# Experts' input of a hybrid decoder: plain column order, two DVE operations a tile

## The chip, the cores and the metric

The kernel runs on one core of one Trainium2 chip. The metric is the device time of one execution in microseconds (us), the median of several runs. The engines are named as in the profile: PE (TensorE), PEld (its weight loads), DVE (VectorE), ACT (ScalarE), POOL or GpSimd, and SP (SyncE), which here only issues DMAs.

## What is computed

One inference step of two trunk layers for 576 tokens of width 1024: 512 of a prompt and 64 of eight samples. The reference, cut to the part around the change:

```python
def trunk(x, c, pos0, s_gla, s_ret, s_ssd, s_conv, p):
    ...
    for l in range(DEPTH):
        mod = jax.nn.silu(c) @ p['w_ada'][l] + p['b_ada'][l]
        sh1, sc1, g1, sh2, sc2, g2 = jnp.split(mod[:, None, :], 6, axis=-1)
        h = x * (1.0 + sc1) + sh1
        mix, st = mixer(h, pos0, s_gla[l], s_ret[l], s_ssd[l], s_conv[l], l, p)
        x = layer_norm(ALPHA * x + g1 * mix, p['ln1_g'][l], p['ln1_b'][l]).astype(x.dtype)
        h = x * (1.0 + sc2) + sh2
        x = layer_norm(ALPHA * x + g2 * hier_moe(h, l, p), p['ln2_g'][l], p['ln2_b'][l]).astype(x.dtype)
    ...
```

`hier_moe` takes `h`, chooses for each token one of four groups and in it two of four experts by router logits, and adds the two experts' `(silu(h @ w1) * (h @ w3)) @ w2`, weighted. `w1` and `w3` are 1024x256, `w2` is 256x1024, all fp32. The change touches how `h`, the experts' input, is made from `x` and how `w1` and `w3` are laid out in SBUF for it.

## The kernel before

The 576 tokens lie in five tiles of rows, `t` = 0 to 3 with 128 prompt rows each and `t` = 4 with the 64 sample rows, taken in the order 4, 0, 1, 2, 3. A layer has four stages: the mixer (phase A), then phase B with the second half of the output projection, the layer norm and the router, then the experts in 16 blocks, then the combination.

In phase B each tile goes through these steps. `out_part` multiplies with the output weights on PE, and DVE applies the gate (L1576) and adds the residual with a running sum (L1580). `stat` makes the mean, the variance (ACT squares, L1610; the last tile by DVE's statistics, L1616) and the reciprocal root by DVE on single columns (L360 to L366). `experts_in` makes the experts' input `h`: ACT normalizes (L1632), GpSimd multiplies with one row vector (L1633) and adds another (L1634), each over the tile's 1024 columns; of the last tile, t = 3, ACT and GpSimd take half the columns, and DVE the other half by two fused operations (L1637, L1638). The row vectors, `r2` and `r3` in `rows`, hold the layer norm's and the modulation's factors put together; `load_rows` loads them once for tile 4 and once for the four others, into the same two buffers (`bufs=1`). The result goes into the tile `h2p`, or, for t = 0 and 2, into part of `g1`, and is stored to DRAM in `hbuf` twice by SP (L1640). The views in `experts_in` make the columns of `h` strided: column 8p + k of `x` goes to place 128k + p, so that a 128-column chunk of `hbuf` holds every eighth column.

Beside it the router works: `turn` transposes a tile (PE L1653, ACT copies into `h2T`, L1654), `logits` multiplies with the router's weights (L1660; tiles 0 to 3 straight from `x` with `wm`, tile 4 from its `h2p` with `wr`, loaded at L1513 in the matching layout), `choose` and `weigh` (L1125 to L1138 and L1148 to L1154) pick experts and weights on DVE with operations of some 16 columns, and `hot` (L1161), `rank`, `ranked` (L1696) and `weights` (L1686 to L1690) build tables that say which rows each expert takes. `srci` (L1815) holds these row numbers; the experts' blocks gather their rows of `hbuf` by it (an indirect DMA of GpSimd, L1324). Among all this, `gate` and `slots` operations of the mixer's retention heads (L1008, L1009, L1056) are fitted in.

In the experts, `expert_piece` (L1288) loads `w1`, `w3` and `w2` of a block, 1 MB each, on SP. `w1` and `w3` are loaded with "(p k) n -> p k n": a partition takes eight neighbouring rows of the weight, 8 KB in one piece, which fits the strided order of `h`. The first loads of a layer are issued in phase B, the others as their buffers come free. Some blocks split the weights into a rounded and a rest part on ACT and DVE (L329, L330), seven are used as they are.

The order of the instructions on each engine is set by the tile framework's scheduler from the program's order and its dependencies, with a few places fixed by `tc.issue_after`; each engine runs its list in order.

Of the kernel before, what the change touches and what calls it, by code (L numbers as in the profile page):

```python
# [13 lines left out]
AF = mybir.ActivationFunctionType  # L14
ALU = mybir.AluOpType
# [6 lines left out]
KD = 8  # L22
# [26 lines left out]
ORDER = (4, 0, 1, 2, 3)  # L49
# [112 lines left out]
def _body(nc, tc, a, ctx, dbg):  # L162
    pe, dve, act, pool, sp = nc.tensor, nc.vector, nc.scalar, nc.gpsimd, nc.sync
# [35 lines left out]
    def ps(cols=512, pl=None):  # L199
        if pl is None:  # L200
            turns[0] += 1
            pl = psx if turns[0] % 7 > 4 and not held else psp
        return pl.tile([128, cols], F32, name="ps", tag="ps")
# [170 lines left out]
    def tp_(t):  # L374
        return 128 if t < 4 else 64
# [907 lines left out]
    def expert_piece(l, e, i, w):  # L1283

        nm = ("moe_w1", "moe_w3", "moe_w2")[i]
        src = a[nm][l, e] if isinstance(e, int) else a[nm][l, bass.ds(e, 1)].rearrange("o a b -> (o a) b")
        nk = 2 if i == 2 else KD
        sp.dma_start(w.rearrange("p (k n) -> p k n", k=nk), src.rearrange("(p k) n -> p k n", p=128))  # L1288

    def expert_w(l, e, out):  # L1290

        for i, w in enumerate(out):
            expert_piece(l, e, i, w)
        return list(out)
# [204 lines left out]
    def phase_b(l, gates, nrm, gst, slots, rqk, rv, x, R, tabs, rst, fill):  # L1499
# [10 lines left out]
        load_mod_rows(g1, l, 0, 0)  # L1510
        load_mod_rows(g1, l, 0, 1)
        wr = rp.tile([128, KD, 20], F32, name="wr")
        sp.dma_start(wr, a["wr"][l, 0])  # L1513
        br = rp.tile([128, 20], F32, name="br")
        load_row(br, a["br"][l:l + 1, :])
        tp = mkpool(rst, "tB")
# [68 lines left out]
        rows = {}  # L1585
# [8 lines left out]
        stats, hps = {}, {}  # L1594
# [28 lines left out]
        def experts_in(t):  # L1623

            n, r = tp_(t), int(t == 4)
            mu, rstd, b = stats[t]
            views = [hps[t][:n].rearrange("q k p -> q p k")]
            views += [v[:n].rearrange("q (p k) -> q p k", k=KD) for v in (x[:, t], rows[r, 2], rows[r, 3])]

            c = 128 if t != ORDER[-1] else 64  # L1630
            hv, xv, ra, rb = [v[:, 128 - c:] for v in views]
            act.activation(hv, xv, AF.Identity, scale=rstd, bias=b)  # L1632
            pool.tensor_tensor(hv, hv, ra, op=ALU.mult)  # L1633
            pool.tensor_tensor(hv, hv, rb, op=ALU.add)  # L1634
            if t == ORDER[-1]:
                hv, xv, ra, rb = [v[:, :64] for v in views]
                dve.scalar_tensor_tensor(hv, xv, mu, ra, op0=ALU.add, op1=ALU.mult)  # L1637
                dve.scalar_tensor_tensor(hv, hv, rstd, rb, op0=ALU.mult, op1=ALU.add)  # L1638
            for o in (128 * t, PL + 128 * t):
                sp.dma_start(hbuf[o:o + n], hps[t][:n].rearrange("q k p -> q (k p)"))  # L1640

# [136 lines left out]
        p = ps(256)  # L1778
# [9 lines left out]
        for i, t in enumerate(ORDER):  # L1788
            if i + 1 < NT:
                advance(0, ORDER[i + 1])  # L1790
                nxt = out_turn(ORDER[i + 1], (0, 1))
            out_part(t, turned, ws, False, (lambda: turn((0, 1, 2)[i - 2])) if i > 1 else None)
            turned = nxt
            for _ in range(2):
                next(fill, None)
            if i == 2:
                chosen(0)
                turn(4)
            stat(t)
            experts_in(t)  # L1800
            advance(2)
            if i > 1:
                chosen((4, 1, 2)[i - 2])
            for u in ((), (), (), (0, 4), (1,))[i]:
                ranked(u)
        advance(1000)
        t = ORDER[-1]
# [13 lines left out]
    def experts(last, finish, l, x, R, tabs, slots, rqk, rv, ahead):  # L1821
# [8 lines left out]
        with ExitStack() as sE:  # L1830
# [82 lines left out]
            def load(b, i):  # L1913
                if b not in ids:
                    ids[b] = sp.value_load(tabs[2][0:1, NX + 3 + b:NX + 4 + b], min_val=0, max_val=NE - 1)
                if i == 0:
                    bl[b].w = room(b)
                expert_piece(l, ids[b], i, bl[b].w[i])
# [44 lines left out]
            with tc.If((flags & (LIGHTS | 7 << NXS)) > 0):  # L1963
                for b in LIGHT:
                    with bit(b):
                        e = sp.value_load(tabs[2][0:1, NX + 3 + b:NX + 4 + b], min_val=0, max_val=NE - 1)
                        for i in range(3):
                            expert_piece(l, e, i, w3rd[i])
                        whole(bx[b], w3rd)
                        if b in SECOND:  # L1970
                            second, third = [nc.values_load(tabs[2][0:1, i:i + 1], min_val=0, max_val=2 ** NE - 1) for i in (NX + 1, NX + 2)]
                            with tc.If((second & (1 << b)) > 0):
                                whole(b2[b], w3rd)
                            if b in THIRD:
                                with tc.If((third & (1 << b)) > 0):
                                    whole(b3[b], w3rd)
# [214 lines left out]
    with ExitStack() as sX:  # L2191
        xp = mkpool(sX, "xA")
        x = xp.tile([128, NT, D], F32, name="x")
# [15 lines left out]
    for l in range(L):  # L2209
        with ExitStack() as sL:  # L2210
# [3 lines left out]
            x = xp.tile([128, NT, D], F32, name="x")  # L2214
# [9 lines left out]
            with ExitStack() as rst:  # L2224
                fill = chain(*[ada_steps(*g) for g in MODS_B[l]])
                last, finish = phase_b(l, gates, nrm, gst, slots, rqk, rv, x, R, tabs, rst, fill)
                gst.close()
# [10 lines left out]
            with ExitStack() as sG:  # L2238
                tiles = combine(x, tail, rv, sG, LEADS[l], l + 1 == L)
                next(tiles)  # L2240
                if l + 1 < L:
# [5 lines left out]
                    for t, mu, rstd, b, o, load in tiles:  # L2247
                        n = tp_(t)
# [6 lines left out]
                    for t in ORDER:  # L2255
                        n = tp_(t)
# [3 lines left out]
                else:  # L2260
# [3 lines left out]
                    for t, mu, rstd, b, o, load in tiles:  # L2264
                        n = tp_(t)
# [6 lines left out]
                        for h in range(2):  # L2272
                            c = slice(512 * h, 512 * (h + 1)) if t == 3 else slice(0, D)
# [76 lines left out]
```

## Time and profile before

| what | us |
|---|---|
| median of 3 runs | 1425.58 (1424.96 to 1429.27) |
| profiled execution, its own time | 1436.62 |
| its span | 1434.8 |
| PE busy in the span | 1246.4 (87%) |
| DVE busy | 827.1 (58%) |
| ACT busy | 490.7 (34%) |
| POOL busy | 477.4 (33%) |

The mean granted clock of TensorE was 0.916 of full speed. The shares are averages over all stages; phase B of the first layer lies at about 403 to 474 us, that of the second at 1083 to 1155 us, and in these the shares are others, as the rows further down show. A row of a timeline gives an instruction's start and duration, and in brackets how long the engine was idle before it and which instruction ended that. A group of rows gives the busy time of many alike and their mean duration; a mean well above the shortest of them says that some were held.

### The profile page before, as it was taken

How to read it: one execution, taken by the hardware profiler on the slowest of the kernel's cores; microseconds unless marked ns; L12 is line 12 of the kernel's file. 1: busy time of each engine (PE TensorE's matmuls, PEld its weight loads, DVE VectorE, ACT ScalarE, POOL GpSimd, SP SyncE). 2: the span in 40 equal slices, each digit the busy share in tenths (PEclk: the TensorE clock that was granted, in tenths of full speed). 3: DMA queues.
4: the chain of work that ended last, by engine and by line, in shares of the span. 5: the costliest groups of instructions: out<-in, count | busy, mean ns of one | idle time of the engine just before them, and what ended most of it. 6: DMA issues, size and time to landing. Idle time of an engine off the chain costs nothing. (4 is left out here: it accounts for less than half of the span.)

```text
span 1434.8 us, 21937 instructions
## 1 busy us (share of the span) xinstructions
PE 1246.4 (87%) x8166; PEld 945.6 (66%) x8166; DVE 827.1 (58%) x1871; ACT 490.7 (34%) x909; POOL 477.4 (33%) x389
## 2 busy tenths in 40 slices
PE   4999999998987678989979998899898768998894
PEld 0999677676765455667469977777476536656651
DVE  0577457336879433446776746544687953334457
ACT  0553123332344213444345323333134421333343
POOL 0013112125244455541341312232413443534315
PEclk7899999999987699989999998999998769999897
DMA  9544665856162477986624410014555246776644
GB/s 323 169 148 158 227 231 188 293 204 205 38 193 103 161 278 296 379 319 217 189 95 149 120 60 30 5 60 161 185 191 190 101 175 249 306 289 265 213 148 139
DMA packets 100606, 267.24 MB, mean 186 GB/s; under 512 B 30871, under 2 KB 59449, under 8 KB 81528
## 3 DMA queue, kind: packets, MB, share of 16 engines
q1 hardware_dynamic: 84600, 246.62, 48.6%
q0 software_dynamic: 15872, 18.89, 4.0%
q8 instruction: 77, 1.26, 0.4%
q14 instruction: 57, 0.47, 0.1%
HBM read 246.84 MB, written 47.63 MB: 205 GB/s over the span
## 5 line engine op out<-in xcount | busy, mean ns | idle before, releaser
L403 PE MATMUL ps<-whi,hT 128*128 128x256 f32 (+1 forms) x640 | 190.0, 297 | 7.8 <-ACT hT L494 7.0
L404 PE MATMUL ps<-wlo,hT 128*128 128x256 f32 (+1 forms) x640 | 184.4, 288 | 1.2 <-DVE wlo L330 1.2
L405 PE MATMUL ps<-whi,hT 128*128 128x256 f32 (+1 forms) x640 | 184.1, 288 | 0.2
L403 PEld LDWEIGHTS ps<-whi,hT 128*128 128x128 f32 (+1 forms) x640 | 118.2, 185 | 22.1 <-issue 11.2
L404 PEld LDWEIGHTS ps<-wlo,hT 128*128 128x128 f32 (+1 forms) x640 | 118.2, 185 | 3.8 <-issue 2.1
L405 PEld LDWEIGHTS ps<-whi,hT 128*128 128x128 f32 (+1 forms) x640 | 118.1, 185 | 1.8 <-DVE hT L495 0.9
L1386 POOL DMA_INDIRECT ybuf<-ys,srci x36 | 46.8, 1300 | 134.1 <-issue 53.8
L393 PE MATMUL ps<-hT,whi 128*128 128x288 f32 x512 | 88.7, 295 | 0.0
L330 DVE TENSOR_TENSOR wlo<-wraw,whi 128x2048 fp32r<-128x2048 f32 x30 | 68.6, 2287 | 34.8 <-ACT whi L329 34.6
L330 DVE TENSOR_TENSOR wlo<-w3rd,whi 128x2048 fp32r<-128x2048 f32 x22 | 69.5, 3160 | 24.5 <-ACT whi L329 24.5
L1355 PE MATMUL ps<-whi,xh 128*128 128x256 f32 x384 | 59.0, 299 | 23.3 <-ACT xh L1342 12.7
L393 PEld LDWEIGHTS ps<-hT,whi 128*128 128x128 f32 x512 | 74.7, 188 | 0.4 <-ACT zdt L532 0.4
L1564 PE MATMUL ps<-whi,mh 128*128 128x512 f32 (+1 forms) x160 | 71.5, 447 | 3.7 <-ACT mh L1550 3.7
L266 PE MATMUL ada<-wada,scond 128*32 128x512 f32 x384 | 57.0, 668 | 18.1 <-DMA wada<-w_ada 18.1
L1565 PE MATMUL ps<-wlo,mh 128*128 128x512 f32 (+1 forms) x160 | 70.9, 443 | 0.0
L1355 PE MATMUL ps<-wlo,xh 128*128 128x256 f32 x384 | 60.0, 304 | 11.5 <-DVE wlo L330 11.4
L1355 PEld LDWEIGHTS ps<-whi,xh 128*128 128x128 f32 x384 | 52.0, 202 | 27.1 <-ACT xh L1342 13.6
L1566 PE MATMUL ps<-whi,ml 128*128 128x512 f32 (+1 forms) x160 | 68.3, 431 | 1.8 <-DVE ml L1551 1.8
L843 POOL TENSOR_TENSOR qh<-qx,ex 128x256 f32<-128x256 f32 x32 | 31.3, 1008 | 99.3 <-issue 82.0
L1355 PEld LDWEIGHTS ps<-wlo,xh 128*128 128x128 f32 x384 | 54.0, 210 | 14.8 <-DVE wlo L330 14.6
L329 ACT ACTIVATE whi<-wraw 128x2048 fp32r<-128x2048 f32 x30 | 57.3, 1911 | 12.7 <-PE ps L393 7.7
L1375 PE MATMUL ps<-w3rd,hid 128*128 128x512 f32 x128 | 58.6, 601 | 2.8 <-ACT hid L1366 2.8
(560 smaller groups left out, 2908.8 us busy)
## 6 DMA issues: line engine op xcount, KB each, us to landing
wada<-w_ada SPq DMA_DIRECT2D x48, 1024.0 KB, 5.1
wraw<-moe_w SPq DMA_DIRECT2D x36, 1024.0 KB, 9.3
slots<-moe_w SPq DMA_DIRECT2D x30, 1024.0 KB, 10.1
w3rd<-moe_w SPq DMA_DIRECT2D x30, 1024.0 KB, 12.9
wraw<-w_in SPq DMA_DIRECT2D x22, 1024.0 KB, 5.3
wraw<-w_out SPq DMA_DIRECT2D x8, 1024.0 KB, 4.9
ybuf<-bz SPq DMA_DIRECT2D x8, 512.0 KB
hbuf<-g SPq DMA_DIRECT2D x8, 512.0 KB, 2.6
```

The costliest lines, as they stand in the source:

```text
L266: pe.matmul(acc[32 * q:32 * q + 32, :], sc_[:, k, :], w[:, o:o + 512], start=(k == 0), stop=(k == KD - 1))
L329: split.hi = act.activation(hi[:, :n], raw[:, :n], AF.Copy)
L330: dve.tensor_tensor(lo[:, :n], raw[:, :n], hi[:, :n].bitcast(F32), op=ALU.subtract)
L393: pe.matmul(p[:mw, :], lhs[:, k, m0:m0 + mw], rhs[:, k, 288 * h:288 * (h + 1)], start=(k == 0 and lhs is vh and rhs is hT[0]), stop=(k == ...
L403: pe.matmul(p[:n], hT[0][:, k, xs], vh[:, k, :], start=(k == 0), stop=False)
L404: pe.matmul(p[:n], hT[0][:, k, xs], vl[:, k, :], start=False, stop=False)
L405: pe.matmul(p[:n], hT[1][:, k, xs], vh[:, k, :], start=False, stop=(k == KD - 1))
L1355: pe.matmul(p, x[:, k], v[:, k], start=(x is self.xh and v is vh and k == 0), stop=(x is self.xl and k == KD - 1))
L1375: pe.matmul(p, self.hT[:, f], v[:, f, c], start=(f == 0), stop=(f == 1))
L1564: pe.matmul(p[:n], mh[:, k, :n], vh, start=(k == 0), stop=False)
L1565: pe.matmul(p[:n], mh[:, k, :n], vl, start=False, stop=False)
L1566: o = pe.matmul(p[:n], ml[:, k, :n], vh, start=False, stop=(k == 3))
```

## The change

`experts_in` makes `h` in plain column order, by two DVE operations over the tile's 1024 columns: (x + mu) times the first row vector, then times the reciprocal root plus the second. ACT's L1632, GpSimd's L1633 and L1634 and the two half-width DVE operations go. Since `h` is in plain order, `w1` and `w3` are loaded with "(k p) n -> p k n", where a partition takes eight rows of 1 KB that lie 128 rows apart (`w2` stays as it is), and tile 4's router weights come from the copy in plain layout, of the same size. The names "first two expert weights" in the change's title mean `w1` and `w3` of every expert.

```diff
--- before.py
+++ after.py
@@ -1285,7 +1285,7 @@
         nm = ("moe_w1", "moe_w3", "moe_w2")[i]
         src = a[nm][l, e] if isinstance(e, int) else a[nm][l, bass.ds(e, 1)].rearrange("o a b -> (o a) b")
         nk = 2 if i == 2 else KD
-        sp.dma_start(w.rearrange("p (k n) -> p k n", k=nk), src.rearrange("(p k) n -> p k n", p=128))
+        sp.dma_start(w.rearrange("p (k n) -> p k n", k=nk), src.rearrange("(p k) n -> p k n" if i == 2 else "(k p) n -> p k n", p=128))
 
     def expert_w(l, e, out):
 
@@ -1510,7 +1510,7 @@
         load_mod_rows(g1, l, 0, 0)
         load_mod_rows(g1, l, 0, 1)
         wr = rp.tile([128, KD, 20], F32, name="wr")
-        sp.dma_start(wr, a["wr"][l, 0])
+        sp.dma_start(wr, a["wr"][l, 1])
         br = rp.tile([128, 20], F32, name="br")
         load_row(br, a["br"][l:l + 1, :])
         tp = mkpool(rst, "tB")
@@ -1624,18 +1624,9 @@
 
             n, r = tp_(t), int(t == 4)
             mu, rstd, b = stats[t]
-            views = [hps[t][:n].rearrange("q k p -> q p k")]
-            views += [v[:n].rearrange("q (p k) -> q p k", k=KD) for v in (x[:, t], rows[r, 2], rows[r, 3])]
-
-            c = 128 if t != ORDER[-1] else 64
-            hv, xv, ra, rb = [v[:, 128 - c:] for v in views]
-            act.activation(hv, xv, AF.Identity, scale=rstd, bias=b)
-            pool.tensor_tensor(hv, hv, ra, op=ALU.mult)
-            pool.tensor_tensor(hv, hv, rb, op=ALU.add)
-            if t == ORDER[-1]:
-                hv, xv, ra, rb = [v[:, :64] for v in views]
-                dve.scalar_tensor_tensor(hv, xv, mu, ra, op0=ALU.add, op1=ALU.mult)
-                dve.scalar_tensor_tensor(hv, hv, rstd, rb, op0=ALU.mult, op1=ALU.add)
+            hv = hps[t][:n].rearrange("p k n -> p (k n)")
+            dve.scalar_tensor_tensor(hv, x[:n, t], mu, rows[r, 2][:n], op0=ALU.add, op1=ALU.mult)
+            dve.scalar_tensor_tensor(hv, hv, rstd, rows[r, 3][:n], op0=ALU.mult, op1=ALU.add)
             for o in (128 * t, PL + 128 * t):
                 sp.dma_start(hbuf[o:o + n], hps[t][:n].rearrange("q k p -> q (k p)"))
 
```

The change also moves instructions, since the scheduler orders them anew. On DVE it puts L1628 and L1629 of each tile among the steps of the reciprocal root and the projection's residual. The first place is DVE in layer 0 where tile 0's statistics are ready (`g_3271` is tile 0's place for `h`, `r_3997` its first row vector, `mix` the gated projection, L1655 the router's logits). Before:

```order
L1609 TENSOR_SCALAR stat<-sums 128x1
L1576 TENSOR_TENSOR mix<-ps,g_3271 128x512
L360 TENSOR_SCALAR rq<-stat 128x1
L1580 SCALAR_TENSOR_TENSOR x,sums<-mix,x 128x512
L362 TENSOR_SCALAR rq<-rq 128x1
```

After:

```order
L1629 SCALAR_TENSOR_TENSOR h2p<-h2p,stat,r_3878 64x1024
L351 TENSOR_TENSOR slots<-slots 128x4
L1551 TENSOR_TENSOR ml<-ps,mh 128x512
L352 SCALAR_TENSOR_TENSOR slots<-slots 128x4
L360 TENSOR_SCALAR rq<-stat 128x1
L1628 SCALAR_TENSOR_TENSOR g_3271<-x,stat,r_3997 128x1024
L353 SCALAR_TENSOR_TENSOR slots<-slots 128x4
L362 TENSOR_SCALAR rq<-rq 128x1
L1576 TENSOR_TENSOR mix<-ps,g_3271 128x512
L351 TENSOR_TENSOR slots<-slots 128x4
L363 TENSOR_SCALAR rq<-rq 128x1
L1580 SCALAR_TENSOR_TENSOR x,sums<-mix,x 128x512
```

Tile 4's L1629 and tile 0's L1628 now stand ahead of tile 1's gate L1576 and residual L1580. Tile 4's L1628 stands 29 rows ahead of tile 0's. Tile 2's pair stands ahead of tile 3's last L1580; tile 3's pair stands behind it, where L1637 and L1638 stood.

The second place is ACT in layer 0 around the transposed copies `h2T` of tile 0 (128x512) and tile 4 (128x4x64). Before:

```order
L1610 ACTIVATE g_3271,stat<-x,stat 128x1024
L1654 ACTIVATE h2T<-ps 128x512 x2
L1632 ACTIVATE g_3271<-x,stat 128x128x8
L1854 ACTIVATE x<-x,stat 128x1024
L1654 ACTIVATE h2T<-ps 128x4x64 x2
L1610 ACTIVATE h2p,stat<-x,stat 128x1024
```

After:

```order
L1610 ACTIVATE g_3271,stat<-x,stat 128x1024
L1845 ACTIVATE x<-x,stat 64x1024
L1645 ACTIVATE h2T<-ps 128x512 x2
L1645 ACTIVATE h2T<-ps 128x4x64 x2
L1550 ACTIVATE mh<-ps 128x512
L1610 ACTIVATE h2p,stat<-x,stat 128x1024
```

L1632 of tile 0 and one other operation (`x<-x,stat`, which normalizes `x` in place for the combination) stood between the two tiles' copies; they are next to each other now.

The third place is SP in phase B of layer 0, where tile 0's row vectors (`r`) are loaded. Before:

```order
L1109 DMA ret_p<-slots 128x1x64 x2
L1288 DMA slots<-moe_w 128x2048
L315 DMA r_3998<-mrow_83 128x512 x2
L1640 DMA hbuf<-h2p 64x1024 x2
L315 DMA r_4001<-mrow_83 128x512 x2
```

After:

```order
L1109 DMA ret_p<-slots 128x1x64
L315 DMA r_3997<-mrow_83 128x512 x2
L1109 DMA ret_p<-slots 128x1x64
L1288 DMA slots<-moe_w 128x8x256
L1631 DMA hbuf<-h2p 64x1024 x2
L315 DMA r_4000<-mrow_83 128x512 x2
```

The first row vector's load now stands ahead of one store of the retention state (`ret_p`) and of one weight load, which is also one with 1 KB rows (128x8x256). GpSimd's list is the old one less the twenty rows of L1633 and L1634, and PE's keeps its order but for small moves.

## Rows read from the trace of the kernel before

**Rows 1.** Busy us by stretch: PE, PEld, DVE, ACT, POOL; clock; DMA share; GB/s

```profile
403.00:451.00 48.00, 40.85 (x222) 33.01 (x221) 43.71 (x185) 23.33 (x36) 20.11 (x8) 0.89 0.49 155
451.00:474.20 23.20, 9.90 (x58) 8.04 (x56) 22.53 (x105) 9.09 (x16) 9.09 (x4) 0.60 0.23 91
...
1131.50:1154.70 23.20, 9.50 (x60) 7.51 (x60) 22.42 (x105) 9.45 (x16) 9.11 (x4) 0.65 0.23 91
```

**Rows 2.** DVE, layer 0: start us, us, operation, idle before and releaser

```profile
423.61 0.69 DVE L1580 SCALAR_TENSOR_TENSOR x<-mix,x 128x512 f32<-128x512 f32 x1
...
453.32 2.70 DVE L1580 SCALAR_TENSOR_TENSOR x<-mix,x 128x512 f32<-128x512 f32 x1
...
455.95 2.79 DVE L1154 TENSOR_TENSOR route<-route,e 128x1 f32<-128x1 f32 x1
...
464.25 0.41 DVE L1161 TENSOR_SCALAR gate<-iota,route 128x384 bf16<-128x384 f32 x1
...
469.47 0.17 DVE L1130 TENSOR_TENSOR em<-lg,t 128x16 f32<-128x16 f32 x1
...
472.35 0.15 DVE L1154 TENSOR_TENSOR route<-route,e 128x1 f32<-128x1 f32 x1
472.42 0.22 DVE L1696 TENSOR_TENSOR A<-route,cst 128x64 bf16<-128x64 f32 x1
...
474.10 0.15 DVE L1815 SCALAR_TENSOR_TENSOR srci<-ps,tabs 128x2 int32<-128x2 f32 x1
```

**Rows 3.** GpSimd (POOL), the same columns

```profile
455.56 3.17 POOL L1634 TENSOR_TENSOR g<-g,r 128x1024 f32<-128x1024 f32 x1
```

**Rows 4.** DVE, both layers: groups by line and shape, busy us, mean ns

```profile
L1580 DVE SCALAR_TENSOR_TENSOR x<-mix,x 128x512 f32<-128x512 f32 x16 | 17.2, 1076 | 0.0
...
L1008 DVE TENSOR_TENSOR slots<-slots 128x256 f32<-128x256 f32 x8 | 6.9, 865 | 0.0
...
L1696 DVE TENSOR_TENSOR A<-route,cst 128x64 bf16<-128x64 f32 x8 | 6.9, 862 | 0.0
L1125 DVE SCALAR_TENSOR_TENSOR t<-em,m,cst 128x16 f32<-128x16 f32 x16 | 6.9, 430 | 0.1
L1130 DVE TENSOR_TENSOR em<-lg,t 128x16 f32<-128x16 f32 x8 | 6.5, 817 | 0.1
L1154 DVE TENSOR_TENSOR route<-route,e 128x1 f32<-128x1 f32 x8 | 6.5, 807 | 0.0
...
L1161 DVE TENSOR_SCALAR gate<-iota,route 128x384 bf16<-128x384 f32 x8 | 5.9, 734 | 0.0
L1696 DVE TENSOR_TENSOR A<-route,cst 64x64 bf16<-64x64 f32 x2 | 5.8, 2906 | 0.0
...
L1134 DVE SCALAR_TENSOR_TENSOR em<-route,em 128x16 f32<-128x16 f32 x8 | 3.9, 494 | 0.0
...
L1637 DVE SCALAR_TENSOR_TENSOR h2p<-x,stat,r 128x512 f32<-128x512 f32 x2 | 2.2, 1086 | 0.0
```

**Rows 5.** line L2271: duration ns min/median/max, first, last start

```profile
L2271 DVE SCALAR_TENSOR_TENSOR x<-x,cst,ln x2: 1266/1718/2170, 1416.6 to 1424.8; 128x1024 f32<-128x1024 f32 x2
```

**Rows 6.** waits, 403 to 476 us (total, times, longest); landing of `r`

```profile
PE ps L1660 <- ACT h2T L1654: 4.5, 1, 4.5
...
DMA to landing us min/median/max: 5.8/5.8/5.8
```

**Rows 7.** queue q1, 661 to 665 us (1 KB rows), 548 to 558

```profile
q1 hardware_dynamic: 1346, 1.36, 103.1%
...
q1 hardware_dynamic: 520, 3.83, 91.8%
```

**Rows 8.** PE's waits, 480 to 690 us, the longest entry

```profile
PE ps L1355 <- ACT xh L1342: 6.3, 2, 3.3
```

**Rows 9.** busy time by stretch, columns as in rows 1

```profile
490.00:520.00 30.00, 24.06 (x138) 15.83 (x138) 14.38 (x8) 9.24 (x15) 23.09 (x13) 0.83 0.96 358
...
580.00:610.00 30.00, 29.77 (x212) 20.82 (x207) 14.42 (x13) 14.01 (x19) 16.10 (x12) 1.00 1.02 399
```

## The prediction

> **What bounds the kernel now.** I read the page first, then busy time by stretch, then the two engines' own timelines over the first layer's phase B, then the groups by line over both layers. The change touches one stage of each layer (about 403 to 474 us and 1083.5 to 1155 us) and the weight loads of the expert stage behind it. In the stretch that ends the stage, DVE is busy 22.53 of 23.2 us in layer 0 and 22.42 in layer 1, PE 9.90 and ACT and POOL 9.09 each [rows 1]: DVE sets its end. In the 48 us ahead of it DVE is busy 43.71 and PE 40.85 [rows 1]; there DVE has 4.3 us of slack and either can be the one that is late. The stage ends when DVE writes `srci` at 474.10 [rows 2], which the experts' gather needs.
>
> But DVE's busy time there is not all work. L1154, one multiply of 128x1, takes 2.79 us from 455.95 and 0.15 us at 472.35 [rows 2]. It ends at 458.74; GpSimd's L1634 runs 455.56 to 458.73 [rows 3]. The DVE instruction was held until GpSimd's was done, and the same happens to a DVE instruction wherever one of GpSimd's ten LN operations of a layer runs. The groups over both layers give the size, each less its clean duration [rows 2, 4]: L1580 17.2 - 16 x 0.69 = 6.2 us; L1696 6.9 - 8 x 0.22 = 5.1 and, for 64 rows, 5.8 - 2 x 0.22 = 5.4; L1154 6.5 - 8 x 0.15 = 5.3; L1130 6.5 - 8 x 0.17 = 5.1; L1161 5.9 - 8 x 0.41 = 2.6; L1134, priced clean as L1130, 3.9 - 1.4 = 2.5; L1125, priced as L1696, 6.9 - 3.5 = 3.4; L1008, priced clean as half of L1580 and a little (0.41), 6.9 - 3.3 = 3.6. Together 39.2 us, 19.6 a layer.
>
> **The change part by part.**
>
> *GpSimd's 20 operations go.* 19.6 us of held time leave DVE in each layer, if nothing else of GpSimd takes their place: the order shows that GpSimd loses just those rows. Of this 7.2 us lie in the last stretch, behind the last tile's output projection (one of L1580, 2.70 us at 453.32 [rows 2], so 2.0; one of L1154, 2.6; L1161 and L1134, half of their two layers' 2.6 and 2.5), and 12.4 in the 48 us ahead.
>
> *DVE gets two operations a tile.* Ten of 128x1024 a layer come, and the two half-width ones of 1.09 us go [rows 4]. The nearest row with scalar operand and one tensor each of x and a row vector is L2271, 128x1024: 1.27 us clean, 2.17 for the one that was held [rows 5]. I take 1.27, since GpSimd has nearly nothing left in the stage. Ten cost 12.7 us, less 2.2: +10.5 a layer. Of these, eight operations (tiles 4, 0, 1, 2) stand in the order ahead of the last tile's residual, 10.2 us, and the last tile's pair grows by 0.4 in the last stretch. If each were held once as L2271's second was, it would be 9 us more; nothing in the order would do that to all.
>
> *ACT loses five operations a layer.* ACT is not the bound (9.09 of 23.2 [rows 1]), but in its order one of them and one other stand between tile 0's and tile 4's copies of `h2T`; PE waited 4.5 us there for tile 4's [rows 6]. After, these copies stand next to each other. I count nothing for it, since tile 4's input now comes from DVE and may be as late; up to 4.5 us a layer is the other end.
>
> *The row vectors.* `r2` and `r3` of tiles 0 to 3 are loaded into the buffers that tile 4 used, by SP after the last reader of each. The reader moves from GpSimd to DVE, and DVE now waits itself: L1628 of tile 0 for `r2`, L1629 for `r3`, with the output projection's residual and `ml` queued behind it, and PE behind those. The load takes 5.8 us from issue to landing [rows 6]. L1628 of tile 4 stands 29 rows ahead of L1628 of tile 0 in DVE's order, which hold two residuals and their sums and other 512-wide work, some 7 to 8 us. So it should be there, with a store ahead of it in SP's queue as the only doubt. I take 0, with up to 4 us a layer as the other end.
>
> *Stores of `hbuf` and SP.* The stores keep their order on SP; what they wait for ends with DVE's second operation of a tile rather than GpSimd's. The last one comes 0.4 us later behind the same DVE rows and earlier in all; nothing.
>
> *The weights.* All 64 loads of `w1` and `w3` (32 a layer) turn from 8 KB rows to 1 KB rows, and `wr` keeps its size. A load of 1 KB rows alone on the queue: 1346 packets at 103.1% of 4 us of 16 engines, 66.0 engine-us, 0.049 us a packet, 1024 packets over 16 engines 3.1 us a load [rows 7]. For 8 KB rows: 3.83 MB at 91.8% of 10 us, 146.9 engine-us, so 1.05 MB in 2.5 us [rows 7]. The difference is 0.6 us a load, 38 us of queue time over the kernel. On the path it is nothing as long as loads land before they are used: of PE's waits in the first expert stage the longest entry is one for ACT's `xh`, 6.3 us, and no weight's DMA is among them [rows 8]. The engines' time on DMA is full in two bursts a layer (0.96 of 490 to 520, 1.02 of 580 to 610) [rows 9]. A burst of 30 us at 399 GB/s is some 12 loads, eight of them `w1` or `w3`: at most 8 x 0.6 = 4.8 us late a burst, 19 us over four bursts, if nothing is loaded ahead. I take 0, since nobody waits for a load now.
>
> The rows put a 1 KB row at 3.1 / 2.5 = 1.24 of the time of the same bytes in 8 KB rows. The Trainium skill, page "DMA: Bandwidth & Descriptors", section "Why small descriptors are slow (HBM only)", names a fixed overhead of some 3 cycles a packet beside one for each 32 bytes. By it the ratio would be (35/32) / (259/256) = 1.08, an estimate from that page, a load 0.2 us longer and the four bursts at most 6 us. The trace doesn't agree; the sum goes by the rows.
>
> *Sum.* If DVE sets the pace all through, a layer gains 19.6 - 10.5 = 9.1 us. If PE does ahead of 451 us, only the last stretch counts: 7.2 - 0.4 = 6.8. I take 8.3 a layer, nearer to the first, since DVE is the busier of the two there; 16.6 for both. The profiled run of 1436.62 would become 1420.0; it stood 11 us above the median of 1425.58, and I take the same difference off the median: 1409.
>
> **The rivals.**
>
> *Half of it* (waits at new places). DVE is in order, and every tile now puts two operations of 1.27 us ahead of what PE needs next, and a wait for `r2` of up to 4 us is possible. For: 4.3 us of slack ahead of 451 us is little. Against: the held times that go were longer and stood at the same places. 4 us a layer lost of 8.3: 1425.6 - 8.6 = 1417.
>
> *Nothing to be measured.* What was held ahead of 451 us was covered by PE's projection, while the added 10.2 us are not: less the slack of 4.3 the part ahead grows by 5.9, and the last stretch gives 6.8 back. 0.9 a layer, 1423.8. It needs PE to be the bound ahead of 451, where its 40.85 us of 48 are less than DVE's.
>
> *More.* PE's wait of 4.5 us for `h2T` goes too, and the added operations fall into DVE's slack: 9.1 + 3.5 to 4.3, some 13 a layer, 1400.
>
> *Slower: the weight queue becomes the bound.* If loads land when they are used, each of the 64 puts its 0.6 us on the path: +38 - 16.6 = +21, 1447. The point from which it decides: over 21 us, more than half of the queue time added, must reach PE to make the kernel slower by over 0.3%. Against it: no PE wait names a load [rows 8]. For it: the bursts at full share [rows 9].
>
> *It doesn't do what it says.* If DVE's long durations weren't GpSimd's doing, they would stay, and 10.5 us a layer come on top: 1425.6 + 21 = 1447. The two ends within 0.01 us [rows 2, 3] speak against it.
>
> **How the numbers follow.** The forecast (1403 to 1413) 0.53, half of it 0.18, more 0.11, nothing to be measured 0.09, slower by the queue 0.06, not what it says 0.03. 0.3% is about what a measurement of this kernel can tell from no change, 4.3 us. Faster by more than that: 0.53 + 0.18 + 0.11 = 0.82; within it 0.09; slower 0.09. The range reaches from the more case, 1399, to past the half case, 1421.
>
> **What would show it.** Right: in the profile after, L1154, L1130 and L1696 at 0.15 to 0.25 us each time, L1628 and L1629 at some 1.27 us, `srci` some 8 us earlier in each layer (near 466), and the expert stage as long as before. Wrong on the new operations: L1628 or L1629 well over 1.3 us, or idle time of DVE ahead of L1628 of tile 0 that a DMA of `r` ends. Wrong on the weights: PE waits that name the loads of `wraw`, `w3rd` or `slots`, or the split's ACT or DVE operations starting later after a landing, and a longer expert stage. Wrong on the bound: DVE idle ahead of 451 with PE as releaser, and a gain of 7 us a layer or less.

## The result

The changed kernel takes 1406.58 us, median of 4 runs (1400.76 to 1407.21), against 1425.74 for the kernel before: a ratio of 0.985, 95% interval 0.982 to 0.988, 19.2 us less. The forecast was 1409. Its profiled execution took 1406.39 us with a span of 1404.6, that of before 1436.62, so the two traces stand 30 us apart and the medians 19.

The stages that the change does not touch differ from one execution to the next. Phase B of layer 0 begins (first square, L1610) at 407.0 us in the trace of before and at 402.6 in that of after, and the shift is there already at the first load of expert weights (345.8 and 342.0 us), ahead of all that the change touches. So each kernel is read here by two spans of each layer: the **part ahead**, from the start of the first L1610 to the start of the last residual L1580, and the **last stretch**, from there to the start of `srci`. In us, layer 0 / layer 1:

| kernel | median us | part ahead | last stretch |
|---|---|---|---|
| before | 1425.74 | 46.4 / 47.8 | 20.8 / 20.7 |
| changed | 1406.58 | 43.8 / 42.7 | 13.6 / 13.6 |
| changed, again (e8) | 1406.42 | 43.0 / 43.8 | 13.6 / 13.6 |
| e1: changed, 8 KB rows | 1402.77 | 43.8 / 42.7 | 13.6 / 13.6 |
| e2: before, 1 KB rows | 1424.26 | 46.9 / 46.8 | 20.8 / 20.7 |
| e3: before, both operations on DVE | 1405.89 | 46.7 / 46.8 | 14.9 / 14.9 |
| e4: before without GpSimd's two | 1394.57 | 37.8 / 37.8 | 14.1 / 14.0 |
| e5: changed, first operation twice | 1412.64 | 46.1 / 44.4 | 15.2 / 15.2 |
| e6: changed, idle work on GpSimd | 1427.27 | 50.9 / 50.4 | 16.7 / 16.7 |
| e7: changed, idle work on ACT | 1400.71 | 42.0 / 43.8 | 13.0 / 13.3 |
| e9: before, tile 0's input later | 1423.66 | 53.6 / 53.0 | 15.1 / 15.1 |
| e10: changed, ACT held at `h2T` | 1402.22 | 41.9 / 42.3 | 13.6 / 13.7 |
| e11: changed, less on DVE (4, 0, 1, 2) | 1446.98 | 43.0 / 39.7 | 13.2 / 13.0 |
| e12: changed, less on DVE (0, 1, 2) | 1397.88 | 42.9 / 39.9 | 12.8 / 13.0 |

The last stretch repeats to 0.1 us in the same kernel, the part ahead to about 1, the median to about 4. The two layers together gain 21.8 us of phase B by these spans, close to the 19.2 of the medians.

### The profile page after: what moved, and what is told of

The parts are those of the page before. It is cut to its first block, busy times and chain, and to the rows that moved or that the text cites. A ratio compares the mean times of both kernels' runs of the same rounds, so it can differ in the third digit from the quotient of the medians.

```text
span 1404.6 us, 21920 instructions
## 1 busy us (share of the span) xinstructions
PE 1232.6 (88%) x8166; PEld 933.9 (66%) x8166; DVE 804.7 (57%) x1887; ACT 472.0 (34%) x899; POOL 424.9 (30%) x369
## 5 line engine op out<-in xcount | busy, mean ns | idle before, releaser
L403 PE MATMUL ps<-whi,hT 128*128 128x256 f32 (+1 forms) x640 | 187.6, 293 | 7.9 <-ACT hT L494 7.0
L405 PE MATMUL ps<-whi,hT 128*128 128x256 f32 (+1 forms) x640 | 182.3, 285 | 0.2
L403 PEld LDWEIGHTS ps<-whi,hT 128*128 128x128 f32 (+1 forms) x640 | 116.7, 182 | 21.1 <-issue 10.1
L405 PEld LDWEIGHTS ps<-whi,hT 128*128 128x128 f32 (+1 forms) x640 | 116.4, 182 | 1.8 <-DVE hT L495 0.9
L1386 POOL DMA_INDIRECT ybuf<-ys,srci x36 | 46.8, 1300 | 133.3 <-issue 49.9
L330 DVE TENSOR_TENSOR wlo<-w3rd,whi 128x2048 fp32r<-128x2048 f32 x22 | 68.7, 3122 | 25.7 <-ACT whi L329 25.7
L1355 PEld LDWEIGHTS ps<-wlo,xh 128*128 128x128 f32 x384 | 53.0, 207 | 14.7 <-DVE wlo L330 12.8
L329 ACT ACTIVATE whi<-wraw 128x2048 fp32r<-128x2048 f32 x30 | 57.3, 1910 | 12.4 <-PE ps L393 7.6
L1324 POOL DMA_INDIRECT qk<-hbuf,srci x22 | 26.4, 1199 | 114.8 <-DVE keyj L1198 84.8
```

The lines of the kernel that those rows point to most:

```text
L329: split.hi = act.activation(hi[:, :n], raw[:, :n], AF.Copy)
L330: dve.tensor_tensor(lo[:, :n], raw[:, :n], hi[:, :n].bitcast(F32), op=ALU.subtract)
L403: pe.matmul(p[:n], hT[0][:, k, xs], vh[:, k, :], start=(k == 0), stop=False)
L405: pe.matmul(p[:n], hT[1][:, k, xs], vh[:, k, :], start=False, stop=(k == KD - 1))
L1355: pe.matmul(p, x[:, k], v[:, k], start=(x is self.xh and v is vh and k == 0), stop=(x is self.xl and k == KD - 1))
L1386: st = pool.indirect_dma_start(out=out, in_=rows, in_offset=None, out_offset=bass.IndirectOffsetOnAxis(ap=to, axis=0), bounds_check=n - 1, ...
```

## The profile after

Busy time by stretch, of before and of after, with the stretches cut as above (PE, PEld, DVE, ACT, POOL, granted clock, DMA share, GB/s):

```profile
406.96:453.32 46.36, 39.21 (x215) 31.91 (x214) 42.33 (x183) 25.23 (x37) 20.52 (x9) 0.89 0.51 160
453.32:474.10 20.78, 7.58 (x39) 5.81 (x37) 20.72 (x99) 6.80 (x14) 8.37 (x4) 0.56 0.25 101
1086.45:1134.20 47.75, 41.43 (x211) 33.58 (x209) 42.34 (x182) 25.21 (x37) 20.49 (x9) 0.82 0.47 156
```

```profile
402.61:446.45 43.84, 40.19 (x218) 32.84 (x216) 38.54 (x194) 17.38 (x33) 1.80 (x2) 0.84 0.57 194
446.45:460.09 13.64, 6.02 (x36) 4.37 (x34) 13.61 (x98) 5.06 (x12) 0.00 (x0) 0.58 0.19 77
1069.14:1111.85 42.71, 37.49 (x218) 30.53 (x216) 38.63 (x194) 17.26 (x33) 1.81 (x2) 0.92 0.61 199
1111.85:1125.49 13.64, 5.84 (x36) 4.19 (x34) 13.61 (x98) 5.06 (x12) 0.00 (x0) 0.59 0.19 77
```

The last stretch is DVE's before and after (20.72 of 20.78 us, 13.61 of 13.64) and 7.1 us shorter. GpSimd's 8.4 us there are gone. In the part ahead PE is busy 40.19 of 43.84 us now and DVE 38.54: neither is far from being the bound. DVE's busy time there has fallen by 3.8 us in each layer (42.33 to 38.54, 42.34 to 38.63).

DVE's groups over both layers, the ones that answer to [rows 4], with the two new operations:

```profile
L1580 DVE SCALAR_TENSOR_TENSOR x<-mix,x 128x512 f32<-128x512 f32 x16 | 10.8, 676 | 0.0
...
L1628 DVE SCALAR_TENSOR_TENSOR h2p<-x,stat,r 128x1024 f32<-128x1024 f32 x4 | 5.1, 1278 | 0.0
...
L1629 DVE SCALAR_TENSOR_TENSOR g<-g,stat,r 128x1024 f32<-128x1024 f32 x4 | 5.1, 1271 | 0.0
...
L1125 DVE SCALAR_TENSOR_TENSOR t<-em,m,cst 128x16 f32<-128x16 f32 x16 | 3.6, 224 | 0.0
...
L1008 DVE TENSOR_TENSOR slots<-slots 128x256 f32<-128x256 f32 x8 | 3.3, 412 | 0.0
...
L1161 DVE TENSOR_SCALAR gate<-iota,route 128x384 bf16<-128x384 f32 x8 | 3.3, 410 | 0.0
...
L1687 DVE TENSOR_TENSOR A<-route,cst 128x64 bf16<-128x64 f32 x8 | 1.7, 211 | 0.0
...
L1130 DVE TENSOR_TENSOR em<-lg,t 128x16 f32<-128x16 f32 x8 | 1.3, 168 | 0.0
L1134 DVE SCALAR_TENSOR_TENSOR em<-route,em 128x16 f32<-128x16 f32 x8 | 1.3, 168 | 0.1
...
L1154 DVE TENSOR_TENSOR route<-route,e 128x1 f32<-128x1 f32 x8 | 1.2, 150 | 0.1
```

Each line of [rows 4] that was held has come down to its clean duration: L1154 from 6.5 to 1.2 us, L1130 from 6.5 to 1.3, L1580 from 17.2 to 10.8, L1687 (L1696 of before) from 6.9 to 1.7, and its two rows of 64 partitions from 2.9 us each to 0.21. L1628 and L1629 take 1.27 to 1.28 us. The end of the stage, as in [rows 2]:

```profile
446.45 0.68 DVE L1580 SCALAR_TENSOR_TENSOR x<-mix,x 128x512 f32<-128x512 f32 x1
...
460.09 0.15 DVE L1806 SCALAR_TENSOR_TENSOR srci<-ps,tabs 128x2 int32<-128x2 f32 x1
```

PE's waits in phase B of layer 0 (us in total, times, longest), first the longest of before, where [rows 6] showed 4.5 us for `h2T`:

```profile
PE ps L1699 <- DVE gate L1161: 5.7, 6, 2.0
```

After:

```profile
PE ps L1690 <- DVE gate L1161: 4.0, 4, 2.6
PE ps L1170 <- DVE gm L1127: 3.4, 1, 3.4
...
PE ps L1651 <- ACT h2T L1645: 0.3, 1, 0.3
```

The wait for `h2T` is 0.3 us now. The waits that name DVE's `gate` were there before and went from 5.7 to 4.0 us; the one of 3.4 us for DVE's L1127 is new. What is left of PE's waits names DVE nearly throughout. No wait of DVE names the load of `r`.

The expert stage, from `srci` to the last L1375, took 209.8 and 235.2 us before and 206.8 and 234.6 after. The loads with 1 KB rows, in ten us of it where the queue is full, as in [rows 7], and SP's issues of expert weights in the first layer (ns min/median/max):

```profile
q1 hardware_dynamic: 3016, 3.04, 94.5%
```

```profile
L1288 SPq DMA_DIRECT2D w3rd<-moe_w x15: 345/1657/5021, 476.7 to 629.9; - x15
...
L1288 SPq DMA_DIRECT2D wraw<-moe_w x15: 347/815/6437, 477.9 to 641.0; - x15
...
  ACT whi L329: 2.7, 2
...
DMA to landing us min/median/max: 5.6/12.1/15.2
```

0.945 x 160 engine-us over 3016 packets are 0.050 us a packet, 3.2 us a load. Landing takes 12.1 us in the median (9.9 before), and in the expert stage of the first layer only two ACT operations waited for a load, 2.7 us in all.

## The experiments

**e1 and e2, the weights' rows alone.** e1 undoes them in the changed kernel (the edit below), e2 does them alone in the kernel before (the reverse).

```diff
-        sp.dma_start(w.rearrange("p (k n) -> p k n", k=nk), src.rearrange("(p k) n -> p k n" if i == 2 else "(k p) n -> p k n", p=128))
+        sp.dma_start(w.rearrange("p (k n) -> p k n", k=nk), src.rearrange("(p k) n -> p k n", p=128))
```

> The changed kernel with one part undone: w1 and w3 loaded with 8 KB rows again, while h stays in plain order (so the rows of the weights do not fit h's order; the experts' results differ, the work is the same). Instructions of all engines but the loads stay in place. Theory (DVE sets phase B, loads land ahead of their use): 1406.6 us within 3, the weight rows cost nothing on the path. Rival (part of the gain is eaten by the 1 KB rows): 1390 to 1402, up to 19 us faster than the changed kernel.

> The kernel before with one part done alone: w1 and w3 loaded with 1 KB rows, h still in the strided order (the weights' rows do not fit it, the work is the same). Theory (loads hidden): 1425.7 us within 3; q1's share of the engines up by some 4 percentage points of the span, no wait of PE on a load. Rival (queue binds): 1432 to 1445.

e1: 1402.77 us, ratio to before 0.982 (0.979 to 0.985), which overlaps the changed kernel's 0.982 to 0.988. e2: 0.9993 (0.9972 to 1.0014). The expert stage takes 207.1 and 234.7 us in e1, 208.6 and 236.9 in e2: with either layout what it took without. No cost of the rows shows. e2 bounds it best: the upper end of its interval is 2 us above before. e1 bounds it poorly: its median is 3.8 us below the changed kernel's, and the far ends of the two intervals lie 12 us apart.

**e4, GpSimd's two operations left out of the kernel before.** The row vectors are then missing from the experts' input (of the last tile, from half of it), and with it from what tile 4's router sees.

```diff
             act.activation(hv, xv, AF.Identity, scale=rstd, bias=b)
-            pool.tensor_tensor(hv, hv, ra, op=ALU.mult)
-            pool.tensor_tensor(hv, hv, rb, op=ALU.add)
```

> The kernel before without GpSimd's L1633 and L1634 (the multiplication with and addition of the row vectors is left out except for DVE's half of the last tile). ACT's and DVE's operations stay. Theory (GpSimd's operations hold DVE's): 19.6 us of DVE time a layer go and nothing comes, PE or ACT may become the bound of the part ahead of the last residual; 1390 to 1400 us, DVE's L1154 at 0.15 and L1130 at 0.17 us each time. Rival (the held times were DVE's own): L1154 and L1130 keep their means of 0.81 us and the time stays above 1415.

1394.57 us, ratio 0.977 (0.973 to 0.981), as expected. Stretches and a group of DVE:

```profile
406.46:444.27 37.81, 35.90 (x208) 29.70 (x206) 29.44 (x181) 25.34 (x37) 1.37 (x2) 0.95 0.48 170
444.27:458.36 14.09, 6.35 (x46) 4.59 (x45) 14.01 (x102) 6.50 (x14) 0.00 (x0) 0.65 0.37 147
```

```profile
L1154 DVE TENSOR_TENSOR route<-route,e 128x1 f32<-128x1 f32 x8 | 1.1, 142 | 0.0
```

L1154 is clean (and L1130, 169 ns a time), so it was GpSimd that held it. Of the 12.4 us that were held in the part ahead 9.3 come back (47.1 to 37.8), of the 7.2 in the last stretch 6.7. In the part ahead PE is now busy 35.90 of 37.81 us and DVE only 29.44: PE has next to no slack left, which is the likely reason why the last 3 us of the held time bring nothing. The scheduler also ordered the engines' lists anew in e4.

**e6, the opposite: idle GpSimd work in the changed kernel.**

```diff
             dve.scalar_tensor_tensor(hv, hv, rstd, rows[r, 3][:n], op0=ALU.mult, op1=ALU.add)
+            sc = tp.tile([128, 512], F32, name="sc", tag="sc", bufs=1)[:n]
+            for c in (slice(0, 512), slice(512, D)):
+                for _ in range(2):
+                    pool.tensor_tensor(sc, hv[:, c], hv[:, c], op=ALU.mult)
```

> The changed kernel with idle work on GpSimd: after each tile's second DVE operation four GpSimd multiplications of 512 columns of h by itself into a scratch tile that nobody reads, some 6 us a tile and 30 a layer as GpSimd had before. Theory (GpSimd's operations hold DVE's): DVE's two-input operations get held again for some 15 to 25 us a layer, 1435 to 1455 us. Rival (the gain came from the shorter chain to h): nobody waits for these operations, 1407 within 4.

1427.27 us, ratio to before 1.0004 (0.9978 to 1.0029): the whole gain is gone, though nobody waits for the added operations and DVE, PE and ACT run the same operations in the same order in both layers' phase B. The new order can't be what gave the gain by itself, nor the shorter way to `h`, for both are as in the changed kernel. The time is less than the range expected. Four of GpSimd's operations in the last stretch, the DVE rows beside them, and the stretches:

```profile
462.14 4.52 POOL L1633 TENSOR_TENSOR sc<-h2p 128x512 f32<-128x512 f32 x4 [10.38 <-DVE em L1134]
```

```profile
462.41 1.11 DVE L1161 TENSOR_SCALAR gate<-iota,route 128x384 bf16<-128x384 f32 x1
463.45 1.01 DVE L1125 SCALAR_TENSOR_TENSOR t<-em,m,cst 128x16 f32<-128x16 f32 x1
...
464.67 0.91 DVE L1660 SCALAR_TENSOR_TENSOR lg<-lg,stat,wsum 128x20 f32<-128x20 f32 x1
...
465.65 1.04 DVE L1138 TENSOR_SCALAR route<-t,mm 128x16 f32<-128x16 f32 x1
```

```profile
404.59:455.45 50.86, 41.19 (x217) 33.27 (x216) 49.55 (x193) 17.53 (x33) 21.58 (x18) 0.80 0.49 167
455.45:472.12 16.67, 6.20 (x36) 4.38 (x34) 16.64 (x99) 5.05 (x12) 4.28 (x4) 0.56 0.16 63
```

GpSimd's four run 462.14 to 466.66, 1.13 us each, and in each of them one DVE operation of 128x384 or less is held to its end, about 0.2 us of work (0.4 for L1161) taking 1 us. DVE's busy time grows by 11.0 us in the part ahead and by 3.0 in the last stretch, these by 7.4 and 3.0. What DVE is held for shows in full in the last stretch and by two thirds (0.67) ahead of it. The Trainium skill, page "SBUF — State Buffer", section "Who interferes with whom", says that DVE and GpSimd share a port pair which one holds for its whole instruction while the other is blocked; the traces of before, e4 and e6 agree, with 2.79 us for 0.15 in [rows 2] and these rows.

**e3, both operations on DVE but in the strided order,** with the weights' rows as before.

```diff
-            c = 128 if t != ORDER[-1] else 64
-            hv, xv, ra, rb = [v[:, 128 - c:] for v in views]
-            act.activation(hv, xv, AF.Identity, scale=rstd, bias=b)
-            pool.tensor_tensor(hv, hv, ra, op=ALU.mult)
-            pool.tensor_tensor(hv, hv, rb, op=ALU.add)
-            if t == ORDER[-1]:
-                hv, xv, ra, rb = [v[:, :64] for v in views]
-                dve.scalar_tensor_tensor(hv, xv, mu, ra, op0=ALU.add, op1=ALU.mult)
-                dve.scalar_tensor_tensor(hv, hv, rstd, rb, op0=ALU.mult, op1=ALU.add)
+            hv, xv, ra, rb = views
+            dve.scalar_tensor_tensor(hv, xv, mu, ra, op0=ALU.add, op1=ALU.mult)
+            dve.scalar_tensor_tensor(hv, hv, rstd, rb, op0=ALU.mult, op1=ALU.add)
```

> The kernel before with the other part alone: both operations of every tile on DVE and none on ACT and GpSimd, but h kept in the strided order and the weights in 8 KB rows. DVE's half-width operation in that order took 1.09 us against 1.27 for the whole plain width, so a whole strided one should take 2.17. Theory (DVE sets the pace, held times gone): 10 x 0.9 = 9 us a layer more than the changed kernel, 1424 us, next to no gain over before; L1161, L1154, L1130 as short as in the changed kernel. Rival (the gain came from the shorter chain ACT, GpSimd, GpSimd to h and not from DVE's time): within 4 us of 1407.

1405.89 us, ratio 0.985 (0.981 to 0.989), where 1424 was expected. The kernel to set beside it is e1, which has the same rows of weights: 1402.77, 3 us less, with overlapping intervals. The operation takes 2.04 us, expected were 2.17:

```profile
L1631 DVE SCALAR_TENSOR_TENSOR g<-x,stat,r 128x1024 f32<-128x1024 f32 x4 | 8.1, 2035 | 0.0
```

```profile
402.14:448.84 46.70, 40.79 (x217) 32.99 (x216) 44.15 (x193) 17.51 (x33) 1.81 (x2) 0.82 0.52 182
448.84:463.78 14.94, 5.64 (x36) 3.99 (x34) 14.91 (x98) 5.06 (x12) 0.00 (x0) 0.59 0.18 71
```

The ten cost 7.6 us of DVE a layer more than in plain order. The last stretch is 1.3 us longer, as the last pair's 1.5 would have it, but the part ahead grows by 3.5 only, while DVE's busy time there grows by 5.6 (38.54 to 44.15): 0.63 of it. DVE, PE and ACT run the same operations in phase B in the same order as in the changed kernel, so that this comes nearest to the price of DVE's time alone (PE's clock was 0.82 here, 0.84 and 0.92 in the changed kernel). In phase B e3 is some 9.5 us slower than the changed kernel over both layers, in the median not at all. In the traces the stretch between the two phases B, which the edit does not touch, takes 603.5 us in e3 and 609.1 in the changed kernel; why it differs I can't say. By its time alone e3 would fit its rival, that the gain came from the shorter way to `h`; e6 rules that out, since it keeps the shorter way and has no gain. Taking GpSimd out is the larger share by far, and the expectation had set the price of DVE's work too high.

**e5, more DVE work in the changed kernel:** the first operation of each tile is issued twice.

```diff
             dve.scalar_tensor_tensor(hv, x[:n, t], mu, rows[r, 2][:n], op0=ALU.add, op1=ALU.mult)
+            dve.scalar_tensor_tensor(hv, x[:n, t], mu, rows[r, 2][:n], op0=ALU.add, op1=ALU.mult)
```

> The changed kernel with the first DVE operation of each tile issued twice: 10 x 1.27 = 12.7 us of DVE work a layer more, no other change of the result. Theory (DVE sets the pace all through phase B): +25 us, 1432. Rival (PE sets it ahead of the last residual, DVE only behind): only the last tile's operation counts, +1.3 a layer, 1409.

The expectation counts ten operations a layer where the edit adds five: 6.4 us a layer, so the first theory should have read +12.7, 1419. Measured were 1412.64 us (0.992, 0.988 to 0.996), +6; the interval holds 1419 and comes close to the rival's 1409, so that the time decides between neither. By the spans the last stretch grows by 1.6 and the part ahead by 1.9, for four operations (5.1 us) that add 3.3 us to DVE's busy time there. The order on the engines differs from the changed kernel's, here and in e12.

**e11 and e12, less of it.** In e11 tiles 4, 0, 1 and 2 lose the second operation (its condition is `t == ORDER[-1]`), in e12, which the edit below shows, tiles 0, 1 and 2.

```diff
-            dve.scalar_tensor_tensor(hv, hv, rstd, rows[r, 3][:n], op0=ALU.mult, op1=ALU.add)
+            if t in (4, ORDER[-1]):
+                dve.scalar_tensor_tensor(hv, hv, rstd, rows[r, 3][:n], op0=ALU.mult, op1=ALU.add)
```

> The changed kernel without the second DVE operation of tiles 4, 0, 1 and 2 (the scaling by the reciprocal root and the addition of the second row vector are left out there): 4 x 1.27 = 5.1 us of DVE work a layer less, all ahead of the last residual. If DVE sets the pace there, that part falls from 43 to 38 us and the time to 1396. From the runs with added DVE work (5 to 6 us more there made the part 2 to 3.5 us longer) I expect 40 to 41 us and 1400 to 1403. If PE sets it, no change, 1406.

> The changed kernel without the second DVE operation of tiles 0, 1 and 2 only (their scaling and second row vector are left out; tile 4, from whose input its router works, keeps both, so that the tokens go to the same experts as in the reference): 3 x 1.27 = 3.8 us of DVE work a layer less, all ahead of the last residual. If DVE sets the pace there, the part falls from 43.3 to 39.5 us and the time by 7.6 to 1399. If its work there counts about two fifths, as the runs so far say (5.1 to 6.1 us more made it 1.9 to 3.4 us longer), 41.8 us and 1403. If PE sets it, no change, 1406.

e11's time (1446.98) says nothing: the router of tile 4 works from that input, the tokens went to other experts, and the first layer's expert stage took 253 us. Its part ahead is 43.0 and 39.7 us. e12: 1397.88 us, ratio 0.981 (0.978 to 0.984), some 9 us under the changed kernel, nearest to the 1399 of the theory that DVE sets the pace. The spans don't bear that theory out: the part ahead is 42.9 and 39.9, 1.9 us less in the mean, where the theory has 3.8 (DVE's busy time fell by 2.6). The two layers differ though DVE does the same:

```profile
404.11:447.02 42.91, 40.82 (x217) 33.24 (x216) 36.04 (x195) 17.34 (x33) 1.80 (x2) 0.84 0.61 198
...
1067.28:1107.14 39.86, 36.68 (x217) 30.13 (x216) 35.95 (x196) 17.43 (x33) 1.80 (x2) 0.96 0.67 213
```

DVE is busy 36.04 and 35.95 us, PE 40.82 at a granted clock of 0.84 and 36.68 at 0.96. The 3 us go with PE's clock: the part ahead is as much PE's as DVE's.

**e7 and e10, ACT.** In e7 ACT gets idle work behind each tile, in e10 between the copies of tile 0's and tile 4's `h2T`.

```diff
             dve.scalar_tensor_tensor(hv, hv, rstd, rows[r, 3][:n], op0=ALU.mult, op1=ALU.add)
+            sc = tp.tile([128, 512], F32, name="sc", tag="sc", bufs=1)[:n]
+            for c in (slice(0, 512), slice(512, D)):
+                act.activation(sc, hv[:, c], AF.Identity, scale=rstd, bias=b)
```

```diff
             n = tp_(t)
+            if t == 4:
+                sc = tp.tile([128, 4, 128], F32, name="sc", tag="sc", bufs=1)
+                for i in range(6):
+                    act.activation(sc, turns_[0][:, 4:8], AF.Copy)
```

> The changed kernel with idle work on ACT: after each tile's second DVE operation two ACT Identity operations of 512 columns of h into a scratch tile that nobody reads, some 2.5 us a tile, about what ACT lost in the change. Theory (ACT is not the bound): 1407 within 4. Rival (a part of the gain came from ACT's shorter list, as the copies of h2T that PE waited 4.5 us for): 1411 to 1418.

> The changed kernel with six idle ACT copies of 512 columns into a scratch tile that nobody reads, between tile 0's and tile 4's copies of h2T, 3.5 us, where ACT had L1632 and one other operation before. DVE's and GpSimd's work stay. Theory A (ACT's list counts): PE's wait for h2T comes back with 3 to 4.5 us and the part ahead of the last residual grows from 43 to 45 to 47; 1411 to 1414 us. Theory B: the wait comes back, the part ahead grows by less than 1 us; 1407 within 3.

e7 took 1400.71 us (0.977 to 0.985), e10 1402.22 (0.975 to 0.987); the changed kernel beside e7 had 0.982 to 0.989. This work on ACT costs nothing that shows. In e10 the wait did not come back, ACT's and PE's rows show why:

```profile
413.67 3.95 ACT L1641 ACTIVATE sc<-h2T 128x512 f32<-128x512 f32 x6
417.65 0.66 ACT L1649 ACTIVATE h2T<-ps 128x256 f32<-128x256 f32 x2
```

```profile
417.01 0.71 PE L1648 MATMUL ps<-cst,h2p 64*128 64x64 f32 x8
418.08 0.64 PE L1655 MATMUL ps<-wr,h2T 128*64 128x20 f32 x8 [0.37 <-ACT h2T L1649]
```

The six copies end at 417.6, and PE transposes tile 4 only at 417.01 to 417.72; ACT would have stood idle until then. PE waits 0.37 us. So e10 doesn't tell what that wait was worth.

**e9, the wait for `h2T` taken out of the kernel before,** by issuing tile 0's ACT and GpSimd operations behind tile 4's copies.

```diff
-                act.activation(hT[:, 4 * h:4 * h + 4, :n], p.rearrange("p (k n) -> p k n", k=4)[:, :, :n], AF.Copy)
+                o = act.activation(hT[:, 4 * h:4 * h + 4, :n], p.rearrange("p (k n) -> p k n", k=4)[:, :, :n], AF.Copy)
+            return o
...
             if i == 2:
                 chosen(0)
-                turn(4)
+                with tc.issue_after(turn(4).ins):
+                    experts_in(0)
             stat(t)
-            experts_in(t)
+            if i != 1:
+                experts_in(t)
```

> The kernel before with tile 0's ACT normalization (and with it GpSimd's two operations) issued behind the copies of tile 4's h2T instead of between tile 0's and tile 4's copies; the result is the same, and GpSimd's operations and their held times are as many as before. The profiles so far show the part of phase B ahead of the last residual 47 us long before and 43 after the change, while PE's wait for tile 4's h2T fell from 4.5 to 0.3 us. Theory A (part of the gain ahead of the last residual is ACT's shorter list): that wait falls below 2 us and the part ahead is 2 to 4 us shorter, 1418 to 1422 us. Theory B (all of it is the held DVE time less the added DVE operations): the wait falls, the part ahead stays 47 within 1, 1425 within 3.

```profile
PE ps L1170 <- DVE Os L1173: 8.1, 1, 8.1
...
PE ps L1661 <- ACT h2T L1654: 0.4, 2, 0.3
```

```profile
403.90:457.47 53.57, 41.25 (x218) 32.73 (x216) 47.57 (x190) 25.69 (x38) 25.48 (x10) 0.83 0.41 139
457.47:472.54 15.07, 6.54 (x33) 5.30 (x33) 15.05 (x91) 5.61 (x12) 3.06 (x2) 0.50 0.35 140
```

1423.66 us, ratio 1.0005 (0.998 to 1.003). The wait fell to 0.4 us, and PE waited 8.1 us for DVE instead. GpSimd's operations now fall into the part ahead, 25.48 us of them against 20.52, and it grows from 47 to 53 while the last stretch loses the same; the two together are 68.7 and 68.1 us as before (67.1 and 68.4). Neither theory had that shift. Since the edit moves GpSimd's operations along with the wait, it shows only that the two together are worth nothing, not what the wait alone was worth.

**e8, the changed kernel once more,** beside e5 to e7.

> The changed kernel itself, on the same chip as the three runs beside it, so that these can be compared with it: 1406.6 us within 3.

1406.42 us, as expected.

## Why the prediction was right, and where it was not

- *What bounds the last stretch, and the held times:* right. Each of the nine groups fell to its clean duration; e4 takes GpSimd away and they fall, e6 gives it other work and DVE is held again, in part at other lines.
- *The last stretch:* forecast 6.8 us a layer, measured 7.1. `srci` came at 460.09 us where near 466 was forecast, but of these 14.0 us less than before 4.4 lie ahead of phase B.
- *The price of an added operation:* 1.27 us forecast, 1.27 to 1.28 measured, and L2271 was the right row to take it from.
- *The part ahead:* mis-sized. The sum set held time against added time one for one, 12.4 - 10.2 = 2.2 us if DVE sets the pace and 0 if PE does, and 1.5 was taken of it. Measured: 3.8 a layer (47.1 to 43.3), outside both. DVE's busy time there also fell by 3.8, so the terms themselves were off. Counting each row of the traces from the end of the one before it, the held groups lose 12.7 us there, about as summed; the eight operations take 9.6 and not 10.2, since a row starts some 0.07 us before the last one ends (L1154 and L1696 at 472.35 and 472.42 in [rows 2]); and the other rows come out 0.7 shorter.
- *One for one:* this holds from before to after, but not where DVE's time alone is changed. With the same order of operations e3's added work shows by 0.63 and e6's holds by 0.67 of what they add to DVE's busy time in the part ahead, so a hold and work of the same length cost about the same there. At that share 3.8 us would be worth some 2.5. Where the other 1.3 a layer come from stays open: the order, ACT's list and PE's clock changed as well, and the part ahead repeats to about 1 us only.
- *PE there:* the prediction called DVE "the busier of the two" and left out PE's clock. The part ahead had 0.89 and 0.82 before, 0.84 and 0.92 after; the last section shows what such a difference goes with.
- *ACT, and the wait for `h2T` as the case of more:* the wait went, from 4.5 to 0.3 us, though the prediction thought that tile 4's input might be as late. What that was worth is not shown: e7's work stands behind each tile, in e10 the wait did not come back, and e9 moved GpSimd's operations too. Nothing speaks against the zero, and the 1.3 us above are room for a part of it.
- *The row vectors and the stores:* right, no wait of DVE names the row vectors, and the expert stage is no longer than before. The landing took 5.5 us.
- *The weights:* right as to the path (e1, e2). The price of a load, 3.1 us forecast, was 3.2. The estimate by the Trainium skill, page "DMA: Bandwidth & Descriptors", section "Why small descriptors are slow (HBM only)", 1.08 of the time of 8 KB rows, is not what the queue shows: 3.2 against 2.5 us are 1.28.
- *The range* of 1399 to 1421 held the median and each of its four runs.

The forecast came out 2.4 us above the median. The part ahead gave some 2.3 us a layer more than summed; over two layers that is more than the difference, and what stands against it lies in the stages that differ from run to run. That the total came so close is in part luck: phase B gave 21.8 us where 16.6 were summed, and the medians 19.2.

## What to carry to other kernels

Look for DVE operations whose mean is a multiple of their shortest, and lay GpSimd's rows beside them: if both end at the same instant, GpSimd's time is also DVE's, and moving its work to DVE can pay even where DVE is the bound. Price that move by what it takes off DVE's busy time and what it adds to it, and not by the sum of durations; where a second engine is nearly as busy, as PE is here, expect only a part of the difference. To learn that part, leave the helper's work out once, and once change DVE's work alone with all lists in the same order. Read a gain of some us from spans between two marks in the trace, when the stages around it vary by more.

## What the runs showed of the hardware

**SP is held at its own issues.** Before, the issue of an expert load on SP took 0.33 us in the median and 0.66 at most. With 1 KB rows the median for `w3rd` is 1.66 us and the longest 5.0, for `wraw` 6.4, as the rows of L1288 above show: the next load's issue starts only behind it. It is the 1 KB rows that do it: in e2, the kernel before with these rows, the longest is 6.4 us too, and in e1, the changed kernel without them, it is 0.57. That the issue lasts until the queue has room is a reading that no row here shows. It cost nothing that e1 and e2 could measure; in that stage SP issues only loads.

**PE's clock after a wait.** Three us each of before, layer 0, columns as above; the first two hold the wait for `h2T`:

```profile
422.00:425.00 3.00, 0.26 (x5) 0.12 (x2) 2.79 (x14) 1.96 (x1) 0.00 (x0) 0.98 0.98 198
425.00:428.00 3.00, 1.23 (x9) 1.11 (x9) 2.96 (x4) 2.97 (x6) 2.74 (x1) 0.50 0.89 225
428.00:431.00 3.00, 3.00 (x15) 2.61 (x15) 1.91 (x5) 0.40 (x4) 2.71 (x2) 0.50 0.58 246
```

PE is busy 0.26 and 1.23 us of 3, the granted clock goes from 0.98 to 0.50, the lower of its two levels (1.2 GHz instead of 2.4), and it is still there in the third stretch with PE busy all of it. The same work of the part ahead keeps PE busy 40.82 us at a mean of 0.84 and 36.68 at 0.96 (e12, above). But in the changed kernel, layer 0, the clock also fell, to 0.50 at about 418 us, although PE had been busy 17.92 us of the 18.00 before (399.60 to 417.60), and in layer 1 at the same place it did not; what decides that no run here tells.
